# A decoder block on one core: the split of the compressed values, the gate exponentials and the row masks change their places in the queues

## The chip, the cores and the metric

The kernel runs on one core of one Trainium2 chip. The metric is the device time of one execution in microseconds, the median of three runs. A profile is one further execution with the hardware profiler on; its times are counted from the start of the span.

## The reference

One layer (SEQ 256, D_MODEL 1024, batch 1). A combined projection `h = x @ w_in` feeds two branches, which are gated and merged; then come an output projection, a layer norm, and a ConvGLU feed-forward with a second layer norm. What the change touches:

```python
# branch 1: gated DeltaNet, 8 heads of 128, chunks of C = 64 tokens
q, k, v = split(silu(causal_dwconv(concat([dq, dk, dv]), dn_conv_w)))
q = l2norm(q) * 128 ** -0.5;  k = l2norm(k);  beta = sigmoid(db)
g = -exp(dn_a_log) * softplus(da + dn_dt_bias)           # then cumsum in each chunk
decay = exp(where(j <= i, g[i] - g[j], -inf))
a_mat = strict_lower(beta * k @ k.T * decay) + eye       # solved against v and k
qk = (q @ k.T) * decay                                   # then a scan over the 4 chunks
# branch 2: sparse attention, 8 heads in 2 groups
kc = partial_rope(compress(k_cmp));  vc = compress(v_cmp)   # 15 blocks
# compress: silu(blk @ w1) @ w2
p_cmp = masked_softmax(q @ kc.T * scale);  o_cmp = p_cmp @ vc
o = sig(g0) * o_cmp + sig(g1) * o_sel + sig(g2) * o_win
```

## The kernel before

**Chunks.** The weights of every projection come as chunks of 128 x 1024 float32 (512 KB), in one fixed order: k0-7, q0-7, kc0-1, vc0-1, nq0-3, four cmp chunks, nq4-7, four cmp chunks, ksl0-1, kwn0-1, four cmp chunks, vt0-3, four cmp chunks, then v, z, mgd, mgn, wd and wn (8 each), wo, and the feed-forward. A chunk is split into `hi` (ScalarE, L192) and `lo` (VectorE, L197; for some early chunks POOL takes a part, L199), and multiplied with three matmuls for each of 8 row blocks (L319 to L321: hi x hi, hi x the low part of x, lo x hi). Up to three chunks are held split at a time (`hi`, `lo`, 3 buffers), six raw. The product lands in `pg`, one of two PSUM buffers, and an evacuation on ScalarE or VectorE frees it. The cmp chunks hold the first layer of `compress`; their matmuls are L776.

**Pumps.** Everything else is written as Python generators. After each chunk that `feat` or `vtok` handles, `pump()` advances each living generator by one step, in the order in which they were started; what a generator issues in that step goes into the engines' queues at that place. The engines take their queues strictly in this order. A `yield from self.wait(name)` gives up as many pumps as the tables say: `WAITS["name0"]` for the first time that name is met (name1 for the second), else `W["name"]`. So "z3's pump" is the step after z3's matmuls were issued, and before z4's. `drain(flag)` pumps without chunks until a flag is set. The generators of this case:

- `smalls`: beta, decay and NSA gates. At flag "q" (after q7's chunk) it waits `s1`, issues the exponentials and logarithms of the gates on ScalarE, waits `s2`, issues a chain of small operations to `g` on POOL (L409 to L426), waits `pgm`, and sums `g` in matmuls (`pgm`, L430 to L434). Functions of different tables need a table load (L141); `defer` runs q's silu one pump after its evacuation.
- `delta`: the chunked rule. It waits `ss`, takes the norms' logarithm (`lnr`), the row factors `rcat` and `bL` and four exponentials; waits `rows`, transposes `rcat` (`pr`, L499), copies it (`rrow`, L501), sends it from POOL's queue to DRAM (`rscr`, L504) and back, spread over the rows (`seed`, L507); adds the masks mL and mQ to the column factors on POOL (L514, into `KD`); waits `mask`; for w = 0, 1 shuffles (L519) and adds (L520) on VectorE and exponentiates. Then for each chunk of tokens `psim`, `pk` and two products (L534, L535); the blocks of 16 are inverted on POOL (L577, L579, L582) behind a round trip through DRAM (L567, L569) and ahead of another (L585, L588); then levels of `pa`, `pu`, `pt` (L611, L617, L622) with updates of T and TT (L623, L624), in two halves, and the scan.
- `cmp_end(w)`: waits `ca`, takes the hidden layer (`phs`, L792), its silu by Exp, waits `cb`. For w = 0 the compressed keys `KCC`. For w = 1 it waits `vcc`, repeats the hidden layer six times (`h6`, L820, two POOL copies), multiplies (L824, tile `pc2`, shown as pc) and splits the product into bfloat16 parts (`vh`, `vm`, `rest`), from which `VCC` is put together (L829 to L836) on ScalarE and VectorE by turns.
- `attention`: `soft(n)` for four (query tile, group) pairs: scores (`psc`, `psa`, L869, L881, L882), maxima (L885), exponentials, sums, and scaling of the weights on VectorE and POOL (L902: four tensor_scalars on each). `weigh(n)` repeats the compressed weights (`e6`, in AT[:, 4096:4456]) on POOL, transposes (`ppt`, `pptc` into `PTC`) and multiplies with V and `VCC` (`poa`).

PSUM tiles made by `self.ps` share four buffers. `vh` and `vm` lie in `PTC`, and `h6` in the place of `e6`.

In the kernel before, the steps fall into these pumps: gate exponentials kc0, POOL chain kc1, `pgm` and the start of `delta` nq0, `lnr` nq2, `pr`, `rscr`, `seed` and both masks nq3, the shuffles nq6, `psim` from nq7 to kwn0, `phs` for w = 0 kwn0, `KCC` vt0, the inversion vt0 to vt3, T and TT filled v5, soft0 z0 to z2 (its L902 in z2), soft1 z3 to z5, `h6` and the split of the compressed values z1, weigh0 z4, z7 and mgd2.

Of the kernel before, what the change touches and what calls it, by code (L numbers as in the profile page):

```python
# [10 lines left out]
OP = mybir.AluOpType  # L11
# [54 lines left out]
def plan():  # L66
# [4 lines left out]
    for j in range(NFF):  # L71
        seq += [("ug", j), ("uv", j)]
        if 0 < j <= NFF - TAIL:
# [7 lines left out]
GEMM = [i for i, b in enumerate(PLAN) if b[0] != "cmp"]  # L81
W = dict(p40=1, pgm=2, later=2, rows=1, mask=5, expL=0, expQ=0, vs=2, inv=2, step=1, back=5, lev=1, la=1,
         lb=1, sa=2, sb=1, sc=1, ra=4, rb=3, rc=0, rd=0, lw=0, tw=0, rw=0, ca=2, cb=1, smalls=1, w40=2, t40=1, s1=0, s2=1, wa=1, wb=1,
         wc=0, sv=0, wv=0, lc=0, vcc=5, s3=1, s4=1, ss=0, z=0, on=0, oc=1, sim=1, vb=1, rest=0, zz=1)
WAITS = dict(back0=5, ca0=2, ca1=0, cb0=2, cb1=5, expL0=0, expQ0=1, la0=2, la2=1, la3=3, later0=0, later1=1,
             later3=2, lb0=1, lb1=2, lb2=2, lb3=0, lc0=0, lc1=0, lev0=3, mask0=3, oc0=2, oc1=1, oc2=0, oc3=0,
             on0=0, p400=2, pgm0=3, rb0=11, ra0=1, rest0=2, rows0=1, s10=0, s30=1, s32=1, s34=0, s36=8, s37=0, s41=2,
             s42=3, s43=2, sa2=2, sc0=1, sc2=1, sc3=1, sim0=2, sim2=0, sim3=0, ss0=2, step2=0, sv0=0, t400=1,
             vb0=3, w400=2, wa0=1, wa1=3, wa3=2, wa5=3, wa7=2, wb0=0, wb2=2, wc0=0, wc1=2, wc4=0, wc5=0, wc6=0,
             wv0=4, wv1=0, z0=1, zz0=1)  # L90
PUMPS = {}
# [8 lines left out]
class Body:  # L100
    def wait(self, name, cost=0):
        self.cost += cost
        n = self.seen.get(name, 0)
        self.seen[name] = n + 1
        for _ in range(WAITS.get(f"{name}{n}", W[name])):
            yield
# [357 lines left out]
    def delta(self):  # L464
        nc = self.nc
# [18 lines left out]
        Rk, Rq, bL = rc[:, 0:16], rc[:, 16:32], self.small(16, "bL")  # L484
# [9 lines left out]
        nc.vector.tensor_tensor(ce[:, 0:16], Rk, GL, op=OP.add)  # L494
        nc.vector.tensor_copy(ce[:, 16:32], self.lnb)
        self.act(ce, ce, AF.Exp)
        yield from self.wait("rows")
        pr = self.ps("pr")
        nc.tensor.transpose(pr[0:32, 0:128], rc, self.cp("ident"))  # L499
# [2 lines left out]
        scr = self.dram.tile([2, 32, 64], F32, name="rscr")  # L502
        seed = self.LT[:, 1024:3072]
        nc.gpsimd.dma_start(scr.rearrange("e u t -> u e t"), rrow.rearrange("u (e t) -> u e t", e=2))  # L504
        yield from self.wait("rw")
        for e in range(2):
            nc.gpsimd.dma_start(seed[64 * e:64 * e + 33:32], bass.AP(tensor=scr.tensor, offset=scr.offset + 2048 * e,  # L507
                                                                     ap=[[0, 2], [1, 2048]]))
        bc = lambda t, n, m: t[:, :, None].to_broadcast([128, n, m])
        kd = self.KD.rearrange("p u j -> p (u j)").rearrange("p (w u j) -> p w u j", w=2, u=16)  # L510
        for w, (m, b) in enumerate((("mL", bL), ("mQ", Rk))):
            for hf in range(2):
                us = slice(8 * hf, 8 * hf + 8)
                nc.gpsimd.tensor_tensor(kd[:, w, us], self.cp(m)[:, None, :].to_broadcast([128, 8, 64]),  # L514
                                        bc(b[:, us], 8, 64), op=OP.add)
        yield from self.wait("mask")
        for w, dst in enumerate((L, QKT)):
            flat = dst.rearrange("p u j -> p (u j)")
# [4 lines left out]
        for c in range(4):  # L523
            us = slice(4 * c, 4 * c + 4)
# [49 lines left out]
        for j in range(15):  # L574
            n, m = 15 - j, j + 1
            t = tmp[:, :n * m].rearrange("p (r c) -> p r c", r=n)
# [207 lines left out]
    def cmp_end(self, w, hp):  # L784
        nc = self.nc
        n = 4 * NCMP
        hid = self.small(n, f"hid{w}")
        ex = self.small(n, f"hex{w}")
        yield from self.wait("ca")
        pf = self.ps("phs")[:, :n]  # L790
        for c in range(2):
            nc.tensor.matmul(pf[:, 30 * c:30 * c + 30], hp[:, 128 * c:128 * c + 128], self.cp("sel"),  # L792
                             start=True, stop=True)
        self.act(ex, pf, AF.Exp, scale=-1.0)
        nc.vector.tensor_scalar(ex, ex, 1.0, None, op0=OP.add)
        nc.vector.reciprocal(ex, ex)
        nc.vector.tensor_tensor(hid, pf, ex, op=OP.mult)
        yield from self.wait("cb")
        hv = hid.rearrange("p (c g n) -> p c g n", c=2, g=2)
        w2 = self.pp("w2").rearrange("p (w c d) -> p w c d", w=2, c=2)  # L800
        if w == 0:
            po = self.ps("pc2")
            pk = po[:, :30].rearrange("p (g n) -> p g n", g=2)
            for c in range(2):
                nc.tensor.matmul(pk, w2[:, 0, c], hv[:, c], start=(c == 0), stop=(c == 1))
            nc.vector.tensor_copy(self.KCC, pk)
            kt = self.KCC[0:32]
            sh = self.consts.tile([32, 2, NCMP], F32, name="shc")
            nc.vector.stream_shuffle(sh, kt, [(i + 16) % 32 for i in range(32)])
            for t, m in ((kt, "ccos"), (sh, "csin")):  # L810
                nc.vector.tensor_tensor(t, t, self.cp(m)[0:32][:, None, :].to_broadcast([32, 2, NCMP]), op=OP.mult)
            nc.vector.tensor_tensor(kt, kt, sh, op=OP.add)
        else:
            self.flags.add("cmp")
            yield from self.wait("vcc")
            po = self.ps("pc2")
            rows = 6 * NCMP
            h6 = self.AT[:, 4096:4456].rearrange("p (c g b n) -> p c g b n", c=2, g=2, b=6)
            for c in range(2):
                nc.gpsimd.tensor_copy(h6[:, c], hv[:, c][:, :, None, :].to_broadcast([128, 2, 6, NCMP]))  # L820
            pv = po[0:rows, :256]
            for g in range(2):
                for c in range(2):
                    nc.tensor.matmul(pv[:, 128 * g:128 * g + 128], h6[:, c, g].rearrange("p b n -> p (b n)"),  # L824
                                     w2[:, 1, c], start=(c == 0), stop=(c == 1))
            vh, vm = (self.PTC[0:rows, 256 * i:256 * i + 256] for i in range(2))
            out = self.VCC.rearrange("p g d -> p (g d)")
            rest = self.scr("vr")[0:rows, :256]
            part = self.cp("vm")[0:rows]  # L829
            nc.scalar.copy(vh, pv)  # L830
            nc.vector.tensor_tensor(rest, pv, vh, op=OP.subtract)
            nc.scalar.copy(vm, rest)
            self.act(out, vh, AF.Copy, scale=part[:, 0:1])
            nc.vector.scalar_tensor_tensor(out, vm, part[:, 1:2], out, op0=OP.mult, op1=OP.add)
            nc.vector.tensor_tensor(rest, rest, vm, op=OP.subtract)
            nc.vector.scalar_tensor_tensor(out, rest, part[:, 2:3], out, op0=OP.mult, op1=OP.add)  # L836
            self.flags.add("vcc")

    def attention(self):
        nc = self.nc  # L840
# [65 lines left out]
        def weigh(n):  # L906
            while f"soft{n}" not in self.flags:
                yield
            qt, g = divmod(n, 2)
# [10 lines left out]
            for i2 in range(2):  # L920
                yield from self.wait("wc")
                if qt:
                    for i in (2 * i2, 2 * i2 + 1):
                        pt = self.ps("ppt").rearrange("p (b q) -> p b q", b=4)
                        for b in range(4):
                            nc.tensor.transpose(pt[:, b], E[:, i, b // 2, 128 * (b % 2):128 * (b % 2) + 128], ident)
                        if i % 2:
                            nc.vector.tensor_copy(PT[:, :, i], pt)
                        else:
                            nc.scalar.copy(PT[:, :, i], pt)  # L930
                else:
                    pt = self.ps("ppt").rearrange("p (b i q) -> p b i q", b=2, i=2)
                    for i in range(2):
                        for b in range(2):
                            nc.tensor.transpose(pt[:, b, i], E[:, 2 * i2 + i, b, :128], ident)
                    for b in range(2):
                        nc.scalar.copy(PT[:, 2 * b, 2 * i2:2 * i2 + 2], pt[:, b])
                if i2 == 1:
                    pt = self.ps("pptc")[0:6 * NCMP].rearrange("p (i q) -> p i q", i=4)
                    for i in range(4):  # L940
                        nc.tensor.transpose(pt[:, i], e6[:, i].rearrange("p b n -> p (b n)"), ident)
                    nc.scalar.copy(PTC.rearrange("p (i q) -> p i q", i=4), pt)
                yield from self.wait("wa", 4 * (qt + 1))
            po = self.psum.tile([128, 512], F32, name="poa", tag="c", bufs=1)
            while "vcc" not in self.flags:
                yield
            nc.tensor.matmul(po, self.VCC[:, g], PTC, start=True, stop=False)
            bs = range(4) if qt else (0, 2)
            for b in bs:
# [16 lines left out]
        for n in range(4):  # L966
            yield from weigh(n)
            self.flags.add(f"weigh{n}")
# [540 lines left out]
```

## Time and profile before

| | us |
|---|---|
| median of 3 runs (lowest to highest) | 571.19 (569.96 to 572.04) |
| the profiled execution's own time | 570.68 |
| its span in the profile | 568.9 |
| TensorE (PE) busy | 554.0 |
| VectorE (DVE) busy | 394.4 |
| ScalarE (ACT) busy | 308.2 |
| GpSimd (POOL) busy | 115.0 |

A row of the timeline has the start, the duration (both us), engine, line, operation, output <- inputs, shapes and count; in brackets stands how long the engine had been idle before it, and what ended that. "PE a <- DVE b" in the list of waits gives the total, the number of times and the longest. In a stretch, busy time of each engine is followed by the granted TensorE clock, the DMA share and GB/s. PEld are weight loads.

### The profile page before, as it was taken

How to read it: one execution, taken by the hardware profiler on the slowest of the kernel's cores; microseconds unless marked ns; L12 is line 12 of the kernel's file. 1: busy time of each engine (PE TensorE's matmuls, PEld its weight loads, DVE VectorE, ACT ScalarE, POOL GpSimd, SP SyncE). 2: the span in 40 equal slices, each digit the busy share in tenths (PEclk: the TensorE clock that was granted, in tenths of full speed). 3: DMA queues.
4: the chain of work that ended last, by engine and by line, in shares of the span. 5: the costliest groups of instructions: out<-in, count | busy, mean ns of one | idle time of the engine just before them, and what ended most of it. 6: DMA issues, size and time to landing. Idle time of an engine off the chain costs nothing.

```text
span 568.9 us, 11592 instructions
## 1 busy us (share of the span) xinstructions
PE 554.0 (97%) x4585; PEld 508.2 (89%) x4585; DVE 394.4 (69%) x681; ACT 308.2 (54%) x568; POOL 115.0 (20%) x160
## 2 busy tenths in 40 slices
PE   9999999999998999999999999999999999999994
PEld 6999999878997998878998898899999999999974
DVE  2788744867976654466658486878777777778884
ACT  4656654524484466463777344465655555556651
POOL 2466624018500330003001000078000000000003
PEclk9999999999999999999999999999999999999998
DMA  8985556575852232233354645635655555555501
GB/s 313 407 326 167 171 192 244 196 262 161 247 176 76 75 129 96 75 95 104 105 181 154 217 159 184 249 117 180 214 183 191 190 182 191 185 185 173 200 1 74
DMA packets 28182, 99.94 MB, mean 176 GB/s; under 512 B 3340, under 2 KB 3996, under 8 KB 27740
## 3 DMA queue, kind: packets, MB, share of 16 engines
q1 hardware_dynamic: 27312, 95.94, 49.5%
q0 software_dynamic: 672, 2.93, 1.7%
q8 instruction: 36, 0.59, 0.4%
q10 hardware_dynamic: 144, 0.33, 0.1%
q14 instruction: 18, 0.15, 0.1%
HBM read 97.33 MB, written 1.46 MB: 174 GB/s over the span
## 4 chain that ended last, share of the span: by engine, by line
PE 74%; DVE 8%; ACT 7%; DMA 4%; issue 3%; POOL 3%; SPq 0%; DVEq 0%; ACTq 0%; POOLq 0%
PE pg L319 16%; PE pg L321 16%; PE pg L320 16%; PE pdn L1270 3%; PE pdn L1271 3%; PE pdn L1269 3%; DVE lo L197 2%; ACT hi L192 2%; PE poa L951 2%; POOL VN L579 1%; PE pwo L994 1%; PE pwo L993 1%; PE pwo L992 1%; POOL itmp L577 1%; DMA VN<-tscr 1%
## 5 line engine op out<-in xcount | busy, mean ns | idle before, releaser
L197 DVE TENSOR_TENSOR lo<-raw,hi 128x1024 fp32r<-128x1024 f32 (+1 forms) x147 | 181.7, 1238 | 77.6 <-ACT hi L192 76.2
L192 ACT CAST hi<-raw 128x1024 fp32r<-128x1024 f32 (+1 forms) x151 | 154.7, 1029 | 34.3 <-PE pg L320 11.8
L319 PE MATMUL pg<-X,hi 128*128 128x256 f32 x496 | 143.7, 290 | 0.9 <-ACT V L1048 0.9
L320 PE MATMUL pg<-X,hi 128*128 128x256 f32 x496 | 139.7, 282 | 0.0
L321 PE MATMUL pg<-X,lo 128*128 128x256 f32 x496 | 139.6, 282 | 0.0
L319 PE MATMUL pg<-Y,hi 128*128 128x256 f32 x400 | 113.3, 283 | 0.0
L321 PE MATMUL pg<-Y,lo 128*128 128x256 f32 x400 | 112.6, 282 | 0.0
L320 PE MATMUL pg<-Y,hi 128*128 128x256 f32 x400 | 112.6, 282 | 0.0
L319 PEld LDWEIGHTS pg<-X,hi 128*128 128x128 f32 x496 | 93.5, 188 | 6.1 <-issue 3.1
L320 PEld LDWEIGHTS pg<-X,hi 128*128 128x128 f32 x496 | 93.5, 189 | 0.3 <-issue 0.2
L321 PEld LDWEIGHTS pg<-X,lo 128*128 128x128 f32 x496 | 93.5, 188 | 0.0
L320 PEld LDWEIGHTS pg<-Y,hi 128*128 128x128 f32 x400 | 75.4, 188 | 0.3 <-issue 0.2
L319 PEld LDWEIGHTS pg<-Y,hi 128*128 128x128 f32 x400 | 75.3, 188 | 0.2 <-issue 0.2
L321 PEld LDWEIGHTS pg<-Y,lo 128*128 128x128 f32 x400 | 75.3, 188 | 0.0
L1345 POOL TENSOR_TENSOR NQ<-NQ,AT 128x512 f32<-128x512 f32 x2 | 2.6, 1287 | 159.7 <-ACT NQ L146 159.7
L1270 PE MATMUL pdn<-lo,X 128*128 128x512 f32 (+1 forms) x90 | 31.6, 351 | 0.0
L1269 PE MATMUL pdn<-hi,X 128*128 128x512 f32 (+1 forms) x90 | 31.5, 350 | 0.0
L1271 PE MATMUL pdn<-hi,X 128*128 128x512 f32 (+1 forms) x90 | 31.4, 349 | 0.0
L902 POOL TENSOR_SCALAR AT<-AT,sums 128x128 f32<-128x128 f32 (+1 forms) x12 | 10.9, 918 | 89.3 <-DVE sums L894 46.8
L351 DVE SCALAR_TENSOR_TENSOR uv<-pg,ppk,uv 128x255 f32<-128x255 f32 (+1 forms) x44 | 21.2, 481 | 11.0 <-ACT uv L146 9.8
L351 DVE SCALAR_TENSOR_TENSOR cv<-pg,ppk,cv 128x255 f32<-128x255 f32 (+2 forms) x48 | 23.1, 481 | 8.1 <-ACT cv L146 6.9
L1309 ACT CAST X<-ug 128x256 fp32r<-128x256 f32 x22 | 9.0, 407 | 33.2 <-DVE ug L1305 33.2
(355 smaller groups left out, 943.9 us busy)
## 6 DMA issues: line engine op xcount, KB each, us to landing
raw<-in_w SPq DMA_DIRECT2D x156, 512.0 KB, 3.4
AT<-in_w SPq DMA_DIRECT2D x12, 512.0 KB, 6.3
Z<-in_w SPq DMA_DIRECT2D x4, 512.0 KB, 8.0
AT<-in_first SPq DMA_DIRECT2D x3, 512.0 KB, 6.3
V<-in_xk POOLq DMA_DIRECT2D x1, 1024.0 KB, 6.1
KD<-in_lnp POOLq DMA_DIRECT2D x1, 1024.0 KB, 5.0
AT<-in_lnp SPq DMA_DIRECT2D x1, 1024.0 KB, 8.4
AT<-in_first SPq DMA_DIRECT2D x2, 256.0 KB, 3.2
```

The source lines that it names most:

```text
L192: nc.scalar.copy(hi[:, o:o + n], raw[:, o:o + n])
L197: nc.vector.tensor_tensor(lo[:, :n], raw[:, :n], hi[:, :n].bitcast(F32), op=OP.subtract)
L319: nc.tensor.matmul(pg, hi[:, k], src[:, 0, k], start=(k == 0), stop=False)
L320: nc.tensor.matmul(pg, hi[:, k], src[:, 1, k], start=False, stop=False)
L321: nc.tensor.matmul(pg, lo[:, k], src[:, 0, k], start=False, stop=(k == 7))
L351: nc.vector.scalar_tensor_tensor(dst[:, s:], pg[:, :S - s], cw[:, n - 1 - s:n - s], dst[:, s:], op0=OP.mult, op1=OP.add)
L902: (nc.vector, nc.gpsimd)[b].tensor_scalar(e, e, w, None, op0=OP.mult)
L951: nc.tensor.matmul(po, self.VT[:, b % 2, c0:c0 + 128], PT[:, b].rearrange("p i q -> p (i q)"), start=False, stop=(b == bs[-1]))
L1269: nc.tensor.matmul(p, fh[:, ts], hi[:, sl], start=(j == 0), stop=False)
L1270: nc.tensor.matmul(p, fh[:, ts], lo[:, sl], start=False, stop=False)
L1271: nc.tensor.matmul(p, fl[:, ts], hi[:, sl], start=False, stop=(j == NFF - 1))
L1309: nc.scalar.copy(fh, f)
```

## The change

Five things move; no arithmetic changes.

- The gate exponentials come one pump later (`s10` 0 to 1), behind q7's silu. `pgm` waits one pump less (`pgm0` 3 to 2), and so does `delta` at `ss` (`ss0` 2 to 1), so that its row factors and their round trip come one pump earlier.
- The four POOL additions of the masks are issued earlier: those with mL and `bL` before the transpose `pr`, those with mQ between the write to DRAM and the read back. `mask0` grows from 3 to 4.
- The hidden layer of the compressed keys comes one pump later (`ca0` 2 to 3).
- The compressed values come two pumps later (`vcc` 5 to 7), in three steps of one pump each, and `h6` lies in `misc` in place of AT.
- `weigh` waits for the flag "vcc" ahead of `pptc` instead of ahead of `poa`, since `vh` and `vm` lie in `PTC`.

```diff
-...wc=0, sv=0, wv=0, lc=0, vcc=5, s3=1, ...
+...wc=0, sv=0, wv=0, lc=0, vcc=7, s3=1, ...
-WAITS = dict(..., ca0=2, ..., mask0=3, ..., pgm0=3, ..., s10=0, ..., ss0=2, ...)
+WAITS = dict(..., ca0=3, ..., mask0=4, ..., pgm0=2, ..., s10=1, ..., ss0=1, ...)
@@ delta
         self.act(ce, ce, AF.Exp)
+        bc = lambda t, n, m: t[:, :, None].to_broadcast([128, n, m])
+        kd = self.KD.rearrange("p u j -> p (u j)").rearrange("p (w u j) -> p w u j", w=2, u=16)
+
+        def masks(w, m, b):
+            for hf in range(2):
+                us = slice(8 * hf, 8 * hf + 8)
+                nc.gpsimd.tensor_tensor(kd[:, w, us], self.cp(m)[:, None, :].to_broadcast([128, 8, 64]),
+                                        bc(b[:, us], 8, 64), op=OP.add)
+        masks(0, "mL", bL)
         yield from self.wait("rows")
...
         nc.gpsimd.dma_start(scr.rearrange("e u t -> u e t"), rrow.rearrange("u (e t) -> u e t", e=2))
+        masks(1, "mQ", Rk)
         yield from self.wait("rw")
...
-        for w, (m, b) in enumerate((("mL", bL), ("mQ", Rk))):
-            for hf in range(2):
-                us = slice(8 * hf, 8 * hf + 8)
-                nc.gpsimd.tensor_tensor(kd[:, w, us], ...)
         yield from self.wait("mask")
@@ cmp_end
-            h6 = self.AT[:, 4096:4456].rearrange("p (c g b n) -> p c g b n", c=2, g=2, b=6)
+            h6 = self.misc[:, :360].rearrange("p (c g b n) -> p c g b n", c=2, g=2, b=6)
...
             nc.vector.tensor_tensor(rest, pv, vh, op=OP.subtract)
+            yield
             nc.scalar.copy(vm, rest)
             self.act(out, vh, AF.Copy, scale=part[:, 0:1])
+            yield
             nc.vector.scalar_tensor_tensor(out, vm, part[:, 1:2], out, op0=OP.mult, op1=OP.add)
@@ attention, weigh
                 if i2 == 1:
+                    while "vcc" not in self.flags:
+                        yield
                     pt = self.ps("pptc")[0:6 * NCMP].rearrange("p (i q) -> p i q", i=4)
...
-            while "vcc" not in self.flags:
-                yield
```

More of the change, by code (lines that the diff above doesn't have):

```diff
@@ L83 @@
          lb=1, sa=2, sb=1, sc=1, ra=4, rb=3, rc=0, rd=0, lw=0, tw=0, rw=0, ca=2, cb=1, smalls=1, w40=2, t40=1, s1=0, s2=1, wa=1, wb=1,
[L84 to L88, printed above, removed]
+         wc=0, sv=0, wv=0, lc=0, vcc=7, s3=1, s4=1, ss=0, z=0, on=0, oc=1, sim=1, vb=1, rest=0, zz=1)
+WAITS = dict(back0=5, ca0=3, ca1=0, cb0=2, cb1=5, expL0=0, expQ0=1, la0=2, la2=1, la3=3, later0=0, later1=1,
+             later3=2, lb0=1, lb1=2, lb2=2, lb3=0, lc0=0, lc1=0, lev0=3, mask0=4, oc0=2, oc1=1, oc2=0, oc3=0,
+             on0=0, p400=2, pgm0=2, rb0=11, ra0=1, rest0=2, rows0=1, s10=1, s30=1, s32=1, s34=0, s36=8, s37=0, s41=2,
+             s42=3, s43=2, sa2=2, sc0=1, sc2=1, sc3=1, sim0=2, sim2=0, sim3=0, ss0=1, step2=0, sv0=0, t400=1,
              vb0=3, w400=2, wa0=1, wa1=3, wa3=2, wa5=3, wa7=2, wb0=0, wb2=2, wc0=0, wc1=2, wc4=0, wc5=0, wc6=0,
@@ L508, in delta @@
                                                                      ap=[[0, 2], [1, 2048]]))
-        bc = lambda t, n, m: t[:, :, None].to_broadcast([128, n, m])
-        kd = self.KD.rearrange("p u j -> p (u j)").rearrange("p (w u j) -> p w u j", w=2, u=16)
-        for w, (m, b) in enumerate((("mL", bL), ("mQ", Rk))):
-            for hf in range(2):
-                us = slice(8 * hf, 8 * hf + 8)
-                nc.gpsimd.tensor_tensor(kd[:, w, us], self.cp(m)[:, None, :].to_broadcast([128, 8, 64]),
-                                        bc(b[:, us], 8, 64), op=OP.add)
         yield from self.wait("mask")
```

## The prediction

> **What bounds the kernel now.** I read the page first, then the waits of TensorE in the part that the change touches, then the stretches, and then each queue in order of time around each wait.
>
> ```profile
> PE 554.0 (97%) x4585; PEld 508.2 (89%) x4585; DVE 394.4 (69%) x681; ACT 308.2 (54%) x568; POOL 115.0 (20%) x160
> ```
> ```profile
> PE psa L881 <- DVE LT L623: 2.1, 1, 2.1
> PE pg L319 <- ACT V L1048: 0.9, 1, 0.9
> PE phs L792 <- DVE LT L534: 0.5, 1, 0.5
> PE pr L499 <- DVE rcat L486: 0.4, 1, 0.4
> ```
>
> TensorE is busy 97% of the span, so only its idle time can be won. The second fence lists all of its waits between 55 and 230 us: 2.1 + 0.9 + 0.5 + 0.4 = 3.9 us. Each has a place, and each part of the change aims at one of them. In between, the other engines lag and wait for TensorE by turns; whether a gain survives depends on which of them TensorE meets next.
>
> **Gate exponentials one pump later (s10 1, ss0 1, pgm0 2).**
>
> ```profile
> 64.18 1.28 ACT L141 ACT_TABLE_LOAD   x1
> ...
> 81.91 1.28 ACT L141 ACT_TABLE_LOAD   x1
> ```
> ```profile
> 72.92 0.22 POOL L426 TENSOR_TENSOR g<-sp,ea 128x16 f32<-128x16 f32 x1
> ```
> ```profile
> 73.19 0.40 PE L430 MATMUL pgm<-g,cpk 128*128 128x16 f32 x2
> ```
> ```profile
> 84.06 0.28 PE L499 MATMUL pr<-cpk,rcat 128*32 128x128 f32 x1 [0.41 <-DVE rcat L486]
> ```
>
> Today the exponentials of the gates stand between the silus of q6 and q7, so the Exp/Ln set is loaded, then Silu again (64.18), then Exp/Ln again (81.91). With q7's silu first, both quoted loads go: 2.6 us of ScalarE. The second lies ahead of lnr, which feeds rcat, for which pr waits. ss0 also brings lnr from nq2's pump to nq1's and pr from nq3's to nq2's. Nearly all of the 0.41 us goes; what may remain is the DVE's few small operations behind its split, so 0.3 to 0.4. The price is the POOL chain to g, issued one pump later (2.85 us). Now g ends at 73.14, and pgm's first matmul starts at 73.19: no margin. Two bounds: g slips by the whole 2.85 and pgm waits for it, or nothing, since in the kernel before POOL got to that chain only behind q7's squares, which waited for the silu behind the load at 64.18. The second row is nearer: I put both on the new order and get g within 0.3 us of where it is. I take 0.
>
> **Masks ahead of the round trip (mask0 4).**
>
> ```profile
> 94.51 1.14 POOL L507 DMA_DIRECT2D LT<-rscr  x2 [5.08 <-DMA rscr<-rrow]
> 95.67 2.08 POOL L514 TENSOR_TENSOR KD<-cpk,bL 128x512 f32<-128x512 f32 x2
> 97.70 2.06 POOL L514 TENSOR_TENSOR KD<-cpk,rcat 128x512 f32<-128x512 f32 x2
> ```
> ```profile
> 94.01 1.23 DVE L197 TENSOR_TENSOR lo<-raw,hi 128x1024 fp32r<-128x1024 f32 x1 [1.62 <-ACT hi L192]
> 96.86 3.99 DVE L197 TENSOR_TENSOR lo<-raw,hi 128x1024 fp32r<-128x1024 f32 x1 [1.62 <-ACT hi L192]
> ```
> ```profile
> 103.49 1.06 ACT L146 ACTIVATE LT<-LT 128x1024 f32<-128x1024 f32 x1 [6.66 <-DVE LT L520]
> ```
>
> The four mask operations run 95.67 to 99.76 back to back, and the DVE split that starts among them takes 3.99 us instead of 1.23. Behind it stand the shuffle and the add, then the exponential at 103.49, in front of which ScalarE idles 6.66 us with nq7's evacuation queued behind; ksl1's pg waits for that slot (0.9 us). Afterwards mL's masks run at about 81 (rcat's time, 84.0, less a chunk), beside small DVE operations, and mQ's 2.06 us lie inside the 5.08 us in which POOL waits for rscr anyway, so the seed DMAs are not delayed; the whole round trip is one pump earlier (a chunk takes 2.85: 94.01 to 96.86). No transfer on SP's queue moves. The shuffles keep their place, nq6's pump (one pump off in ss0, one on in mask0). Their split takes 1.23, so they start some 2.7 us sooner: more than 0.9, the wait goes. If mQ's masks catch nq3's split, it ends up to 2.1 us later; its chunk is multiplied two chunks (5.7 us) later, which hides it.
>
> **The k side's hidden layer one pump later (ca0 3).**
>
> ```profile
> 114.68 1.23 DVE L197 TENSOR_TENSOR lo<-raw,hi 128x1024 fp32r<-128x1024 f32 x1 [1.58 <-ACT hi L192]
> 115.83 0.68 DVE L534 TENSOR_TENSOR LT<-psim,LT 128x512 f32<-128x512 f32 x1
> ```
>
> phs is the fifth user of four PSUM buffers in kwn0's pump and waits for L534. One pump on the buffers are free: 0.5 us goes. Its product KCC is first read by psc in z0's pump, some 40 us later; nothing waits.
>
> So TensorE is 0.4 + 0.9 + 0.5 = 1.8 us ahead. What it meets is the inversion on POOL:
>
> ```profile
> 144.47 1.68 POOL L582 COPY VN<-VN 128x256 f32<-128x256 f32 x1
> ```
> ```profile
> 144.43 1.22 DVE L197 TENSOR_TENSOR lo<-raw,hi 128x1024 fp32r<-128x1024 f32 x1
> ```
> ```profile
> 156.38 1.76 ACT L146 ACTIVATE LT<-VN,cpk 128x256 f32<-128x256 f32 x4 [1.51 <-DMA VN<-tscr]
> ```
>
> ScalarE waits 1.51 us for the inverse to come back, so what follows on ScalarE and DVE keeps POOL's time. The inversion starts from a split in kwn0's pump (114.68, it waits for TensorE's chunk), so it moves by 0.4 + 0.9 = 1.3; the 0.5 comes later. Its last copy, 1.68 us, ran under a split (1.22); the splits move 0.5 us further than POOL does, and the copy may come out up to 1 us shorter. Bounds 1.3 and 2.3; I take 2.0, since copy and split started together and a small shift parts them.
>
> **Values' split two chunks on, in steps (vcc 7, h6 in misc).**
>
> ```profile
> 174.25 0.41 DVE L831 TENSOR_TENSOR vr<-pc,PTC 90x256 f32<-90x256 f32 x1
> 175.54 0.48 DVE L834 SCALAR_TENSOR_TENSOR VCC<-PTC,cpk,VCC 90x256 bf16<-90x256 bf16 x1 [0.89 <-ACT VCC L146]
> 175.95 0.41 DVE L835 TENSOR_TENSOR vr<-vr,PTC 90x256 f32<-90x256 f32 x1
> 176.39 0.48 DVE L836 SCALAR_TENSOR_TENSOR VCC<-vr,cpk,VCC 90x256 bf16<-90x256 f32 x1
> 176.80 0.41 DVE L885 TENSOR_REDUCE mx<-psa 128x2 f32<-128x256 f32 x1
> ...
> 180.19 1.23 DVE L197 TENSOR_TENSOR lo<-raw,hi 128x1024 fp32r<-128x1024 f32 x1 [2.25 <-ACT hi L192]
> ```
> ```profile
> 170.07 1.10 PE L824 MATMUL pc<-ppk,AT 128*90 128x128 f32 x8
> 171.01 0.60 PE L881 MATMUL psa<-KC,NQ 128*128 128x256 f32 x2
> ```
> ```profile
> 183.59 2.08 PE L617 MATMUL pu<-A,LT 64*64 64x64 f32 x64
> 185.51 1.10 PE L622 MATMUL pt<-LT,A 64*64 64x64 f32 x32
> ```
> ```profile
> 184.63 3.17 POOL L902 TENSOR_SCALAR AT<-AT,sums 128x128 f32<-128x128 f32 x4 [30.60 <-DVE ec L895]
> ```
> ```profile
> L820 POOL COPY AT<-hid x2: 347/856/1364, 152.4 to 152.7; 128x180 f32<-128x180 f32 x2
> ```
>
> Counting pumps, the split stands in z1's now (pc between pt and psa at 170.07 agrees) and moves to z3's, its second and third steps to z4's and z5's. In z1 psa finds a free buffer: the 2.1 us go. DVE goes from its T and TT updates to mx directly: 176.80 - 174.25 = 2.5 us off its chain.
>
> But h6 goes too. Its two POOL copies (L820) ran at 152.4, long before pc. POOL takes its instructions in order, and in z2's pump soft0's scaling, four tensor_scalars (L902), is issued; the copies now stand behind them, and pc behind the copies, and TensorE's whole queue behind pc. L902 begins when DVE's sums are ready. That chain (mx, exponentials, z2's evacuation, its hi and lo, A, V, V, A, sums) runs on ScalarE and DVE by turns, one waiting for the other (180.19: DVE for hi), never for TensorE, so it moves by 2.5 + 2.0 = 4.5: L902 begins at 184.63 - 4.5 = 180.1, ends 3.17 later at 183.3, the copies (2 x 0.35) at 184.0, pc's eight matmuls (171.01 - 170.07 = 0.94) at 184.95. Then TensorE is where it now is after half of the 64 matmuls pu: 183.59 + (185.51 - 183.59)/2 = 184.55. So it is 0.4 later than before, after having been some 4.8 ahead (1.8 + 2.1 + pc's 0.94): it reaches pc at about 179.7 and stands there 4.2 us.
>
> Bounds of this term: with POOL's shift between 1.3 and 2.3, +0.1 to +1.1. The rest of the split (L834 to L836, 0.48 + 0.41 + 0.48 = 1.4 us of DVE, and two ScalarE operations) falls into z4 and z5, where TensorE waits for nothing; what it delays is soft1's scaling, first read in mgd2's pump, and weigh0 reaches pptc at z7 only, after the flag. misc is overwritten only from mgd0's evacuation on. I take these at nothing; without that cover they cost the 1.4.
>
> Sum: all four waits go, one of 4.2 us comes, and the net is +0.4, with leftovers of pr +0.5. The profiled execution took 570.68 (span 568.9), so it would take 571.2; the median of the three runs, 571.19, is 0.5 above the profiled one, so the forecast for the median is 571.7: no change that can be told.
>
> [...] L902's third operation ran into the DVE split of z3:
>
> ```profile
> L902 POOL TENSOR_SCALAR AT<-AT,sums x4: 597/647/1329, 184.6 to 187.2; 128x128 f32<-128x128 f32 x4
> ```
>
> One took 1329 ns, the others about 0.6. [...]
>
> **The rivals.** First, faster: the copies cost TensorE no wait, because the sums come earlier than I work out or the lag is smaller; then 3.9 us go and 567.3 is the time. For it: POOL is idle 30.60 us ahead of L902. Against it: POOL's order.
>
> Second, slower: the new stall lets the clock fall.
>
> ```profile
> 156.00:175.00 19.00, 16.93 (x204) 15.65 (x203) 13.37 (x28) 13.69 (x26) 0.00 (x0) 1.00 0.45 146
> ```
> ```profile
> 556.00:562.00 6.00, 4.92 (x42) 4.72 (x40) 3.19 (x8) 0.34 (x1) 4.82 (x4) 1.00 0.14 53
> 562.00:565.00 3.00, 0.00 (x0) 0.00 (x0) 2.93 (x9) 0.50 (x2) 0.00 (x0) 0.94 0.18 70
> 565.00:569.00 4.00, 0.00 (x0) 0.00 (x0) 0.50 (x1) 0.00 (x0) 0.00 (x0) 0.50 0.34 131
> ```
>
> TensorE's last matmul ends at 556 + 4.92 = 560.9; the granted clock (0.94 of 3 us, then 0.50) fell to half at about 564.6, 3.7 us later. The wait of 2.1 us did not bring it down (1.00 in the stretch 156 to 175). A stall of 4.2 us is past that point; if the clock then stays low as long as it took to fall, TensorE loses half of 3.7: 573.5. It decides at 3.7 us of stall. [...]
>
> Third: the change does less than it says. If POOL's chain to g or the mask work makes a new wait in the head, or the inversion moves by 0.5 only, the stall at pc ends 1.5 us later, 571.7 + 1.5 = 573.2.
>
> **How the numbers follow.** Forecast 0.56, first rival 0.20, second 0.17, third 0.07. A change under 0.3% (1.7 us) can't be told from none. Faster is the first, 0.20; slower the second and third, 0.24; same the forecast, 0.56, whose own range is 571.1 to 572.6 by the bounds of its last term, with pr's leftovers and the measurement's spread to each side. To hold 8 in 10, the range goes down to 567.6, leaving out over half of the first rival's spread (0.13), and up to 573.9, past the second and third, leaving out 0.07.
>
> **What would show it.** Right: two loads fewer on ScalarE; L197 at 1.2 us near 97; the four waits gone from TensorE's list, one of about 4 us at pc L824 released by POOL's h6; L902 ahead of the copies near 180. Wrong: pc without a wait of over 2 us, a wait at pgm, the copies ahead of L902, or a clock under 1.00 after pc.

## The result and the profile after

| | before | after |
|---|---|---|
| median (lowest to highest), 4 runs each, us | 571.38 (569.96 to 572.04) | 577.11 (575.70 to 578.98) |
| profiled execution, its span, us | 570.68, 568.9 | 575.70, 573.9 |

The ratio is 1.0106, 95% interval 1.0068 to 1.0144: slower by 5.7 us, above the whole range predicted.

The list of TensorE's waits between 55 and 240 us, after (total, times, longest):

```profile
PE pc L827 <- POOL misc L823: 2.8, 1, 2.8
PE pa L614 <- ACT LT L146: 1.7, 1, 1.7
PE pg L319 <- DVE Z L351: 1.6, 1, 1.6
```

All four waits of before are gone, as forecast, and the one at pc has come, released by POOL's copies. The other two were not forecast: the first `pa` of the levels, and z0's chunk behind it. Together 6.1 us of waits stand for 3.9.

The details of the head came out as forecast. From the page, the timeline of DVE and that of POOL and TensorE around pc (start, duration):

```profile
PE 557.3 (97%) x4585; PEld 512.2 (89%) x4585; DVE 393.4 (69%) x681; ACT 305.3 (53%) x566; POOL 114.4 (20%) x160
```
```profile
95.92 1.22 DVE L197 TENSOR_TENSOR lo<-raw,hi 128x1024 fp32r<-128x1024 f32 x1 [1.62 <-ACT hi L192]
```
```profile
183.66 3.50 POOL L907 TENSOR_SCALAR AT<-AT,sums 128x128 f32<-128x128 f32 x4 [30.57 <-DVE ec L900]
187.12 0.61 POOL L823 COPY misc<-hid 128x180 f32<-128x180 f32 x2
```
```profile
187.50 1.80 PE L827 MATMUL pc<-ppk,misc 128*90 128x128 f32 x7 [2.83 <-POOL misc L823]
```

ScalarE has two instructions fewer (566 for 568: the table loads), the split that took 3.99 us takes 1.22, and soft0's scaling (now L907) stands ahead of the copies. But it begins at 183.66, not at the 180.1 forecast.

TensorE's busy time rose from 554.0 to 557.3 us with the same 4585 instructions. The stretches show why. Their bounds are set at the changes of the granted clock in this trace, and steps of 3.41 us from them; behind the three numbers before the last two columns stands PEclk:

```profile
152.93:156.34 3.41, 3.26 (x28) 3.06 (x26) 0.76 (x1) 0.00 (x0) 0.16 (x1) 1.00 0.95 217
156.34:159.76 3.42, 1.15 (x32) 1.04 (x32) 1.95 (x6) 2.85 (x6) 0.00 (x0) 1.00 0.25 96
159.76:163.17 3.41, 2.50 (x12) 2.54 (x13) 3.30 (x7) 2.75 (x5) 0.00 (x0) 0.50 0.14 31
163.17:166.58 3.41, 3.41 (x18) 3.41 (x18) 1.64 (x2) 2.27 (x3) 0.00 (x0) 0.50 0.67 237
...
183.65:187.06 3.41, 1.01 (x32) 0.88 (x31) 2.74 (x6) 1.29 (x2) 3.40 (x4) 1.00 0.02 5
187.06:190.48 3.42, 2.98 (x28) 2.70 (x30) 0.42 (x1) 0.37 (x1) 2.22 (x9) 0.50 0.50 153
```

Look at the pairs: a stretch in which TensorE was busy 1.15 or 1.01 of 3.41 us, and behind it one in which PEclk is 0.50 (half clock). Neither was idle whole. Three stretches ran at half clock.

Why is the fill of T and TT late? It starts in this row of ScalarE, at 156.91, where before it stood at 156.38 and 154.4 was forecast:

```profile
156.91 1.71 ACT L146 ACTIVATE LT<-VN,cpk 128x256 f32<-128x256 f32 x4 [4.96 <-DMA VN<-tscr]
```

The round trip ahead of the inversion, on POOL's queue, before and then after:

```profile
120.70 1.24 POOL L567 DMA_DIRECT2D lscr<-VN  x1 [20.95 <-DVE hex L795]
125.45 0.57 POOL L569 DMA_DIRECT2D VN<-lscr  x1 [3.51 <-PE pc L805]
128.66 0.22 POOL L577 TENSOR_TENSOR itmp<-VN 128x15 f32<-128x15 f32 x1 [2.63 <-DMA VN<-lscr]
```
```profile
118.62 1.23 POOL L570 DMA_DIRECT2D lscr<-VN  x1 [26.23 <-DVE VN L575]
125.23 0.57 POOL L572 DMA_DIRECT2D VN<-lscr  x1 [5.37 <-PE pc L808]
129.91 1.02 POOL L580 TENSOR_TENSOR itmp<-VN 128x15 f32<-128x15 f32 x1 [4.11 <-DMA VN<-lscr]
```

The write goes out 2.08 us earlier, as forecast, but the inversion starts 1.25 us later. (The brackets of the read back name pc, but in both traces it starts 0.5 us behind the landing of the write, at 124.9 and 124.7.) From the view of DMA issues while the write was under way (KB, median us to landing), before and then after; each is followed by SP's chunk loads in the timeline:

```profile
lscr<-VN POOLq DMA_DIRECT2D x1, 128.0 KB, 4.2
```
```profile
123.27 0.33 SPq L170 DMA_DIRECT2D raw<-in_w  x1
123.69 0.38 SPq L239 DMA_DIRECT2D AT<-in_w  x1
```
```profile
lscr<-VN POOLq DMA_DIRECT2D x1, 128.0 KB, 6.1
```
```profile
119.97 0.33 SPq L170 DMA_DIRECT2D raw<-in_w  x1
120.39 0.38 SPq L239 DMA_DIRECT2D AT<-in_w  x1
```

The loads moved 3.3 us, the write only 2.1. So the two loads of 512 KB now start 1.35 us after the write's issue, not 2.57.

The theory to test: (1) the write and the read back are slowed by the chunk loads beside them, so the inversion and all that hangs on ScalarE and DVE behind it is late; (2) the copies behind the scaling make the wait at pc; (3) a stretch in which TensorE is busy less than half costs a stretch at half clock. The rivals stand with each run.

### The profile page after: what moved, and what is told of

Read it like the earlier page. It is cut to its first block, busy times and chain, and to the rows that moved or that the text cites. A ratio compares the mean times of both kernels' runs of the same rounds, so it can differ in the third digit from the quotient of the medians.

```text
span 573.9 us, 11598 instructions
## 1 busy us (share of the span) xinstructions
PE 557.3 (97%) x4585; PEld 512.2 (89%) x4585; DVE 393.4 (69%) x681; ACT 305.3 (53%) x566; POOL 114.4 (20%) x160
## 4 chain that ended last, share of the span: by engine, by line
PE 57%; DVE 7%; ACT 5%; issue 2%; POOL 1%; DVEq 0%; ACTq 0%; POOLq 0%
PE pg L319 12%; PE pg L320 12%; PE pg L321 12%; PE pdn L1275 3%; PE pdn L1274 3%; PE pdn L1276 3%; ACT hi L192 2%; PE poa L956 1%; DVE lo L197 1%; PE pwo L998 1%; PE pwo L999 1%; PE pwo L997 1%; ACT AT L146 1%; PE pg L1226 1%; DVE ST L687 1%
## 5 line engine op out<-in xcount | busy, mean ns | idle before, releaser
L197 DVE TENSOR_TENSOR lo<-raw,hi 128x1024 fp32r<-128x1024 f32 (+1 forms) x147 | 178.8, 1218 | 76.8 <-ACT hi L192 75.9
L319 PEld LDWEIGHTS pg<-X,hi 128*128 128x128 f32 x496 | 94.5, 191 | 6.7 <-issue 3.1
L320 PEld LDWEIGHTS pg<-X,hi 128*128 128x128 f32 x496 | 94.6, 191 | 0.3 <-issue 0.2
L907 POOL TENSOR_SCALAR AT<-AT,sums 128x128 f32<-128x128 f32 (+1 forms) x12 | 12.3, 1038 | 95.0 <-DVE ec L900 49.1
```

The costliest lines, as they stand in the source:

```text
L197: nc.vector.tensor_tensor(lo[:, :n], raw[:, :n], hi[:, :n].bitcast(F32), op=OP.subtract)
L319: nc.tensor.matmul(pg, hi[:, k], src[:, 0, k], start=(k == 0), stop=False)
L320: nc.tensor.matmul(pg, hi[:, k], src[:, 1, k], start=False, stop=False)
L907: (nc.vector, nc.gpsimd)[b].tensor_scalar(e, e, w, None, op0=OP.mult)
```

## The experiments

**One part at a time.** e1 has the values' split alone, e2 the head alone.

```diff
e1: -ca0=3 mask0=4 pgm0=2 s10=1 ss0=1   +ca0=2 mask0=3 pgm0=3 s10=0 ss0=2, masks behind the seeds
e2: -vcc=7, h6 in misc, yields, PTC's wait   +vcc=5, h6 in AT, no yields, wait ahead of poa
```

> The values' split as in the kernel after; gate exponentials, masks and the k side's hidden layer as in the kernel before. Theory (late inversion and late pc each open a wait, and each wait lets the clock fall): pa and z0's pg have no wait, the clock is 1.00 until z2, the four old waits but psa stay (1.8 us), L902 begins some 2.5 us sooner than before, and pc waits 3 to 5.4 us, with one or two windows of 3.41 us at half clock behind it: 573.5 to 576 us. Rival (the waits alone set the time, the clock adds nothing): net of pc's wait against psa's 2.1 and pc's own place 0.9, +0 to +2.4: 571.4 to 573.8.

> Gate exponentials, masks and hidden layer as after; the values' split as in the kernel before. Theory: the read back of the inversion's blocks lands as late as in the kernel after, pa waits about 1.7 us and z0's pg about 1.6, the clock is at half for two windows (6.8 us) from about 159.8, and psa's wait shrinks or goes, since TensorE is late: 574 to 576.3 us. Rival (the moved split alone is to blame): no wait at pa, clock 1.00, 1.8 us won: 569.6.

e1: 575.41 us, ratio 1.0064 (1.0039 to 1.0088). e2: 572.74 us, 1.0021 (1.0004 to 1.0038). The longest wait of e1, then the waits of e2:

```profile
PE pc L827 <- POOL misc L823: 3.8, 1, 3.8
```
```profile
PE pg L319 <- DVE Z L351: 3.4, 1, 3.4
PE psa L884 <- DVE LT L626: 0.8, 1, 0.8
PE pa L614 <- ACT LT L146: 0.7, 1, 0.7
```

e1 came out as the theory had it but for a wait of 0.7 us at z0's pg: the moved split by itself loses, by 3.8 us at pc. In e2 the head, whose three waits (0.4, 0.9 and 0.5) were all won, loses them again at pa and z0's pg, 4.1 us; so its rival (1.8 us won) falls, but 572.7 is under the range expected: only one stretch, not two, ran at half clock (from 162.52 to 165.94, behind one with TensorE busy 0.87 us).

**The copies out of POOL's order.** e3 issues the two copies ahead of the wait vcc.

```diff
             self.flags.add("cmp")
+            h6 = self.misc[:, :360]...;  for c in range(2): nc.gpsimd.tensor_copy(h6[:, c], ...)
             yield from self.wait("vcc")
```

> The kernel after, with the two POOL copies of the hidden layer issued before the wait vcc, so that they no longer stand behind soft0's scaling. Theory: pc's wait of 2.8 us and the half clock behind it (1.7 us) go, the two waits before z1 and their half clock stay: 577.1 - 4.5 = 572.6 us, 571.8 to 573.4. Rival 1 (the clock adds nothing): 574.3. Rival 2 (pc's wait only gives way to another, DVE's or ScalarE's lag behind TensorE): 575.5 to 577.

572.64 us, 1.0010 (0.9993 to 1.0027), on the 572.6 expected. The wait at pc is gone, the two others stay:

```profile
PE pg L319 <- DVE Z L351: 2.8, 1, 2.8
PE pa L614 <- ACT LT L146: 1.4, 1, 1.4
```

**TensorE kept busy.** e4 puts matmuls that nobody reads into the three waits.

```diff
+    fill(12) ahead of the first pa;  fill(11) ahead of z0's chunk;  fill(20) ahead of pc
```

> The kernel after, and in the three places where TensorE waits, matmuls of X that nobody reads: 12 ahead of the first pa, 11 ahead of z0's chunk, 20 ahead of pc (about 0.12 us each, so 1.4, 1.3 and 2.4 us beside waits of 1.7, 1.6 and 2.8). Theory (the clock is what costs): the granted clock stays at 1.00 from 150 to 200 us, and the time falls by 3.4 + 1.7 = 5.1: 572.0 us, 571.2 to 572.8. Rival (the waits cost, the clock is only their sign): 577, or more by what of the 5.1 us of matmuls isn't hidden.

574.55 us, 1.0051 (1.0034 to 1.0069). The clock stayed at 1.00 from 150 to 200 us (its mean was 0.996, for 0.987 in the kernel after), but only about half of the 5.1 us came back: a miss for both. Its waits, and POOL's copies:

```profile
PE pg L324 <- DVE Z L356: 1.2, 1, 1.2
PE pc L835 <- POOL misc L830: 1.2, 1, 1.2
```
```profile
186.82 0.61 POOL L830 COPY misc<-hid 128x180 f32<-128x180 f32 x2
```

The copies end at 187.4; after they ended at 187.7. Counted from where the two traces stand at 60 us, that is 0.5 us sooner. They hang on the fill and the chain of ScalarE and DVE behind it, hardly on TensorE's speed. So in the kernel after the first two stretches at half clock were mostly covered by the wait at pc: without them TensorE only waits there longer. What the clock cost was mainly the stretch behind pc.

**The round trip.** Both kernels have the copies early (e3). e5 lets SP wait for the write by a small read, e6 issues the read back itself on SP's queue; both hold the chunk loads until the write has landed.

```diff
e5: +        nc.sync.dma_start(hold[0:16], sl[:, 0])
e6: -        nc.gpsimd.dma_start(vf[:, 256:512], sl...)   +        nc.sync.dma_start(vf[:, 256:512], sl...)
```

> The kernel of e3 (copies early), and on SP's queue, between the write of the inversion's blocks (lscr) and the chunk loads that follow, one small read of lscr into a tile that nobody uses: SP waits for lscr, so the chunk loads start only when it has landed (about 123 instead of 120 us). Theory (the write and the read back are slow because chunk loads share the DMA engines with them): lscr lands 4.2 us after its issue, as in the kernel before, instead of 6.1 to 6.7; the read back, now beside the loads, takes 3.1 to 4.5; T and TT are filled some 2 us sooner; the waits at pa and z0's pg fall from 4.2 to 2.2 or less, and where they stay under 1.7 the clock stays at 1.00: 569.0 us, 568 to 570.5. Rival (POOL's queue or the DRAM write itself is slow when it is issued there): lscr still takes about 6 us, and the time is 572.6 or more.

> The kernel of e3, with the read back of the inversion's blocks issued from SP's queue instead of POOL's, which also holds the chunk loads behind lscr's landing. Theory: lscr lands in 4.2 us, the read back starts at about 123 and runs ahead of the chunk loads, landing at 126 instead of 129.8 to 131.8; T and TT are filled some 3.5 us sooner; no wait at pa, none at z0's pg, clock 1.00 until the end: 568 us, 567 to 570. Rival (what follows, DVE's updates of T and TT and the softmax chain, is late by itself): the waits come back at psa or a chunk's pg, and the time is 570 to 571.5. Rival 2: the held chunk loads come too late for TensorE: a wait at pg for raw, hi or lo near 130 us, 571 or more.

e5: 571.70 us, 0.9988 (0.9966 to 1.0009). e6: 566.41 us, 0.9908 (0.9890 to 0.9927). Issues during e5's write, then e6's issues and its timeline of SP and of POOL:

```profile
lscr<-VN POOLq DMA_DIRECT2D x1, 128.0 KB, 4.8
```
```profile
lscr<-VN POOLq DMA_DIRECT2D x1, 128.0 KB, 4.1
VN<-lscr SPq DMA_DIRECT2D x1, 128.0 KB, 2.1
```
```profile
123.49 0.33 SPq L572 DMA_DIRECT2D VN<-lscr  x1
123.91 0.38 SPq L170 DMA_DIRECT2D raw<-in_w  x1
```
```profile
125.76 0.22 POOL L580 TENSOR_TENSOR itmp<-VN 128x15 f32<-128x15 f32 x1 [5.15 <-DMA VN<-lscr]
```

The write took 4.1 to 4.8 us where the loads were held or started 2.6 us behind its issue (before, e1, e5, e6), and 5.8 to 6.7 where they started 1.35 us behind it (after, e2, e3). So the collision of the write is shown by taking it away; whether the two meet in the DMA engines or in DRAM was not told apart. For the read back, the queue and the loads beside it were changed together: in no run does it stand on POOL's queue without loads, so what each does to it stays open. In e5 the read back was still on POOL's queue and beside the loads (3.7 us); z0's pg kept a wait of 1.9 us in the trace, just over half a stretch, and the median misses the 568 to 570.5 expected. Its executions fall in two groups: the four with the highest mean clock (0.995 to 0.998) took 567.6 to 570.0 us, the other eight (0.990 to 0.994) 571.1 to 574.2. In e6 the inversion starts at 125.76, 4.1 us sooner than after, and one wait of 0.3 us is left of the list:

```profile
PE pg L319 <- DVE Z L351: 0.3, 1, 0.3
```

e6 beats both kernels. How much of that is the round trip and how much the change? e9 is the kernel before with the read back on SP, e10 the head alone with it, and e8 the kernel after with it and the copies late.

```diff
-        nc.gpsimd.dma_start(vf[:, 256:512], sl...)
+        nc.sync.dma_start(vf[:, 256:512], sl...)      # in the kernel after (e8), before (e9) and e2's (e10)
```

> The kernel after with the read back on SP's queue as in e6, but with the two POOL copies of the hidden layer where the kernel after has them, behind soft0's scaling. So the inversion is early and only pc's release is late. Theory: in e6 TensorE came to pc at 179.9 us and POOL's scaling ended at 183.8; with the copies behind it (2 x 0.33) pc waits until 184.4, 4.5 us, and at least one window at half clock follows (1.7 us, two windows in about a third of the cases): 566.4 + 4.5 + 1.7 = 572.6 us, 571 to 574.5. Rival 1 (the wait is taken back, because the other engines catch up in it): 568 to 569. Rival 2 (no clock): 570.9.

> The kernel before with nothing but the read back of the inversion's blocks on SP's queue. Theory: there lscr already lands in 4.2 us; the read back lands some 1.5 us sooner (about 127 instead of 128.5), ScalarE's 1.51 us ahead of T and TT go, psa's wait of 2.1 us shrinks to about 0.6 and with it the half clock that some of the runs of the kernel before have; the other waits (0.9, 0.5, 0.4) stay: 570.0 us, 569 to 571.5. Rival (the read back's place alone explains e6's gain): 567.

> e6 without the moved split of the values: gate exponentials, masks and hidden layer as after, read back on SP's queue, values' split (and its copies) as in the kernel before. Theory: TensorE and the fill of T and TT are both some 2.6 us ahead of the kernel before, so psa's wait stays at 2.1 to 2.6 us (with a half window in about half of the runs): 569.3 us, 568.5 to 571; the moved split is then worth about 3 us. Rival (the moved split gains nothing once the copies are out of the way): 566.4.

e8: 571.68 us, 0.9990 (0.9978 to 1.0003). e9: 569.41, 0.9943 (0.9931 to 0.9956). e10: 568.03, 0.9920 (0.9902 to 0.9937), somewhat under its range; psa's wait is 1.9 us there. e9 fits its theory. e10 lies between its theory (569.3) and its rival (566.4). e8 lies in the theory's range, but as near to rival 2 (570.9, no clock) as to the 572.6; its trace has two stretches at half clock behind pc, and what they cost is measured below (e13, e14). In e8's timelines of POOL and TensorE the forecast's own picture stands:

```profile
180.81 3.57 POOL L907 TENSOR_SCALAR AT<-AT,sums 128x128 f32<-128x128 f32 x4 [30.71 <-DVE ec L900]
184.32 0.61 POOL L823 COPY misc<-hid 128x180 f32<-128x180 f32 x2
```
```profile
184.71 2.01 PE L827 MATMUL pc<-ppk,misc 128*90 128x128 f32 x8 [4.15 <-POOL misc L823]
```

| medians, us | copies behind the scaling | copies early |
|---|---|---|
| read back on POOL, beside the loads | 577.1 (after) | 572.6 (e3) |
| read back on SP, loads held | 571.7 (e8) | 566.4 (e6) |

The late copies cost 4.5 or 5.3 us, the round trip 5.4 or 6.2: nearly independent. These medians come from different batches, in which the kernel before stood between 571.4 and 572.6, so their differences are good to about 1 us; the pair that was measured together (e12 and e14, below) gives 5.4 for the late copies. With the round trip mended, the head is worth 1.4 us (e9 to e10, one batch). The moved split with early copies adds 1.6 by the medians of e10 and e6, but only 0.7 by their ratios to the kernel before, whose intervals overlap: that it gains is not shown by itself. Together it is 2 to 3 of the 3.9 us of waits that the change was to win.

**The clock.** e7 is the kernel before with seven stalls, each a matmul that waits for POOL operations which wait for a matmul.

```diff
+    ahead of wd1, wd3, wd5, wd7, wn1, wn3, wn5 (n = 1, 2, 1, 2, 3, 1, 2):
+        matmul(p, ident, t[:, 0:16])
+        for _ in range(n): nc.gpsimd.tensor_scalar(t[:, :512], t[:, :512], 1.0, None, op0=OP.mult)
+        matmul(p, ident, t[:, 0:16])
```

> The kernel before, with seven added stalls of TensorE where it is otherwise without waits: ahead of chunks wd1, wd3, wd5, wd7, wn1, wn3 and wn5 a matmul waits for 1, 2, 1, 2, 3, 1 and 2 POOL operations of 512 columns (about 1.3, 2.4, 1.3, 2.4, 3.4, 1.3 and 2.4 us, by masks of 1.04 us each). Theory (in windows of 3.41 us that run freely, one in which TensorE is busy less than half brings a window at half clock): no half clock behind the 1.3s; behind a 2.4 in (2.4 - 0)/3.41 = 0.70 of the cases; behind the 3.4 always; so about 3 half windows of 5.1 us, and a mean clock some 0.009 under that of the kernel before. Rival (only a window that is idle whole): at most one half window, behind the 3.4, and mostly none. The time: 15 us of stalls, less what others of its waits they hide, and 1.7 us for each half window.

607.06 us, 1.0612 (1.0589 to 1.0635). The stalls were longer than planned: 1.65, 3.28, 1.70, 3.76, 5.17, 1.70 and 3.58 us, 20.8 together, between neighbouring matmuls of the trace. All seven were followed by half clock, the one of 5.17 by two stretches. The mean clock of the profiled execution was 0.971 over 607.8 us, for 0.996 over 568.9 before: 15.3 us more lost to the clock, the worth of nine stretches at half, so one of them stood elsewhere. Eight times 1.7 and 20.8 make 34.4 of the 35.1 us measured. Stretches of e7, placed as above:

```profile
295.86:299.27 3.41, 1.76 (x16) 1.66 (x15) 0.83 (x2) 3.40 (x3) 1.49 (x1) 1.00 0.87 252
299.27:302.69 3.42, 3.42 (x18) 3.42 (x17) 1.23 (x1) 1.70 (x2) 0.00 (x0) 0.50 0.14 55
306.10:309.51 3.41, 1.85 (x8) 0.80 (x6) 2.83 (x5) 2.54 (x5) 1.40 (x1) 1.00 0.55 172
309.51:312.93 3.42, 1.70 (x14) 1.70 (x15) 2.03 (x9) 2.66 (x11) 1.58 (x2) 1.00 0.36 140
```

And the one at psa's wait of 2.1 us in the profile of the kernel before, behind which the clock stayed:

```profile
172.09:175.50 3.41, 1.71 (x13) 1.57 (x14) 2.57 (x4) 0.85 (x3) 0.00 (x0) 1.00 0.35 119
```

Of the stretches at full clock on this grid, half clock followed those with TensorE busy 0.52 us (e7), 0.87 (e2), 1.01 and 1.15 (after), 1.56 (e14), 1.66 (e1) and 1.70 and 1.76 (e7), and did not follow those with 1.71 (before), 1.85 (e7), 1.90 (e2) and 2.22 (e4). The rival, a stretch idle whole, falls. The way back is harder: behind a stretch at half clock, the clock stayed at half where TensorE had been busy 1.42 us (e1), 1.58 (e14) and 2.50 (after) and came back where it had been busy 2.98 and 3.41 (after) and 3.42 (e14). So a wait that reaches into the next stretch can cost two, as it did in e1 and e14.

What does it cost at pc? e11 is e8 with 32 unread matmuls in the wait; e12, e13 and e14 are e6, e11 and e8 again in one batch, since e8 and e11 came from two, in which the kernel before stood at 572.63 and 571.35.

```diff
e11: +            self.fill(32)      # ahead of pc, in the kernel of e8
```

> The kernel of e8 with 32 matmuls of X that nobody reads ahead of pc, 3.8 to 4.1 us of TensorE work inside its wait of 4.2 us. Everything else is the same, so the difference to e8 is the price of the half clock alone. Theory: pc's wait falls to under 0.5 us, no window is under half busy, the clock stays at 1.00 until the last matmuls, and the time is the 571.7 of e8 less one or two half windows (1.2 to 2.5 us by e8's profile, whose two windows moved TensorE's queue by 2.5 us beyond the wait and pc's own place): 569.0 to 570.5 us. Rival (the half clock hides behind the other engines, as part of it did in e4): 571.0 to 571.9.

> The kernel of e6 once more, on one chip with the next two, which have pc's wait without and with the half clock. 566.4 us, 565.5 to 567.5, by e6.

> The kernel of e11 on the same chip: TensorE spends the time of pc's wait on matmuls that nobody reads. Above e12 by the wait alone: 4.2 us by e8's list, less what the others catch up: 3 to 4.2, so 569.5 to 570.6.

> The kernel of e8 on the same chip: pc's wait of 4.2 us idle. Theory (the half clock behind the wait costs TensorE its own share, 1.2 us for one window and 2.6 for two, as the traces of e8 and e11 have it): 1.2 to 2.6 us above e13. Rival (the other engines catch up in the half clock, and it costs next to nothing, as the ratios of e8 and e11 to the kernel before, 0.999 and 0.998, would have it): 0 to 0.6 above e13.

e11: 569.68 us, 0.9981 (0.9962 to 1.0000). On one chip: no wait 566.36 us, 0.9909 (0.9888 to 0.9930); wait filled 569.90, 0.9978 (0.9964 to 0.9992); wait idle 571.76, 1.0001 (0.9982 to 1.0020). So the wait is worth 3.5 us and the half clock behind it 1.9, between one stretch and two (1.6 by the means of the 12 executions each, give or take 1.0). The stretches of the idle one, with two at half clock in this execution:

```profile
177.61:181.02 3.41, 1.56 (x37) 1.29 (x35) 3.31 (x11) 1.32 (x2) 2.07 (x2) 1.00 0.24 93
181.02:184.43 3.41, 1.58 (x7) 1.58 (x8) 0.47 (x1) 0.00 (x0) 3.22 (x10) 0.50 0.48 154
184.43:187.85 3.42, 3.42 (x61) 3.14 (x61) 0.42 (x1) 0.37 (x1) 0.40 (x2) 0.50 0.00 0
```

## Why the prediction was wrong

**What held.** The four waits went; two table loads went; g did not slip, and pgm did not wait; the masks left the split at 1.22 us; KCC was in time; the inversion's last copy took 0.64 us for 1.68. TensorE was even further ahead than the 1.8 us summed: matching its instructions one by one, 2.7 us at 150 us (counted from where the two traces stand at 60 us). The order on POOL, scaling ahead of copies ahead of pc, was as worked out, and where the inversion comes early (e8) the wait at pc is the 4.2 us forecast.

**The step that failed: the shift of the inversion on POOL, "Bounds 1.3 and 2.3; I take 2.0".** It counted when the write is issued and took the time until it lands as given; of POOL's operations only the copy beside a DVE split, 1.68 us, was weighed. The write did go out 2.1 us sooner, but the chunk loads on SP's queue moved by 3.3 and ran into it: write and read back took 11.2 us from issue to landing for 7.8. The inversion began 1.25 us late and the fill 0.5 us late, while TensorE was 2.7 us early. That opened the waits at pa and z0's pg and put the scaling at 183.66 instead of 180.1. In the head's part "no transfer on SP's queue moves" was said of the masks' round trip; for the one of the inversion, the chunk loads were not looked at. Mending this step alone (e8) brings 577.1 to 571.7, in another batch.

**The second step: the clock, put among the rivals and at a wrong threshold.** The clock fell behind pc, as one of the prediction's own signs of being wrong had it. "It decides at 3.7 us of stall" came from the end of the program, where the idle time has no other side (the last matmul ends at 560.9, the clock falls at 564.6); and 4.2 us were past even that, so the fall was no matter for a rival. By e7, about half a stretch, 1.7 us, is enough, if it lies in one. In the traces of the kernels before and after, all changes of the clock lie 3.41 us or multiples of it apart. On such a grid a wait of 4.2 us leaves at least 2.1 us of idle time in one stretch, with TensorE busy 1.3 at most, and the clock fell behind 1.56 in e14 and 1.66 in e1; so it was sure to cost one, and 1.9 us belonged into the likeliest case (e13 to e14). Such a stretch need not be idle whole: TensorE was busy 1.15 and 1.01 us of it in the kernel after and 1.76 in e7.

**A coincidence.** e8's 571.7 is the time forecast, but by errors that cancel: without the half clock it is 569.9 (e13), under the forecast, and the clock brings back 1.9. That its trace meets the working is luck in part, too. In e8 (times here are counted from where the traces stand at 60 us) the scaling begins at 179.9 where 180.1 was forecast, but behind an inversion that began 3.5 us sooner, not 2.0, and a fill that came 2.2 us sooner; in e13 and e14 the fill came 4.3 and 4.1 us sooner, and the scaling began at 178.5 and 178.8.

**Rivals.** The first (faster, no wait at pc) needed what e6 has, copies early and the inversion in time, and gives 566.4 where it was priced at 567.3. The second named the right mechanism; in the kernel after it met at 2.8 us of wait, not at 3.7, and its 573.5 left out the late inversion. The third (the inversion moves by 0.5 only) had the right place and the wrong sign.

## What to carry to other kernels

Work that is brought forward brings the loads behind it forward too (here by 3.3 us, where the write ahead of the inversion came 2.1 us sooner): of a round trip through DRAM on the path, look at what the other queues will have in flight when it runs, or put the read back on the queue of the loads, where it holds them (in e6 it is issued at 123.49, the first load behind it at 123.91). An instruction moved later in one engine's order stands behind all that this engine was given in between (in the kernel after, the copies at 187.12 behind 3.50 us of scaling); issue it where its inputs are ready. The wait of TensorE at pc, 4.2 us by e8's list and 3.7 by e14's, cost 3.5 us where it was filled (e12 to e13) and 1.9 more where it was idle (e13 to e14), with two stretches of 3.41 us at half clock in e14's trace behind one with TensorE busy 1.56 us; in e4 most of what the clock would have cost was covered by a later wait. Of a new wait, look at how much of each such stretch it empties.

## What the runs showed of the hardware that was not expected

- The clock falls not only behind an idle stretch of 3.41 us: it fell behind stretches with TensorE busy up to 1.66 us (e1) and behind 1.70 and 1.76 (e7), and did not behind 1.71 (before), 1.85 (e7) or 1.90 (e2). It came back behind stretches with 2.98 us (after) and more, and did not behind 2.50 (after).
- The half clock was nearly free where TensorE would wait later anyway: in e4, with the clock at 1.00 ahead of pc, POOL's copies, which release pc, ended at 187.4 for 187.7 in the kernel after, or 0.5 us sooner counted from where the traces stand at 60 us.
- A write of 128 KB to DRAM from POOL's queue landed in 4.1 to 4.8 us where two chunk loads of 512 KB started 2.6 us behind it or later (before, e1, e5, e6), and in 5.8 to 6.7 where they started 1.35 us behind it (after, e2, e3); its read back landed in 2.1 us from SP's queue ahead of the loads (e6) and in 3.1 (before), 3.7 (e5) and 4.5 (after) from POOL's beside them.
